# A 90-degree rotation of 96 images: slabs 1 and 2 loaded in 8 KB lines and stored in 16 KB lines

## The chip, the cores and the metric

The kernel runs on one core of a Trainium2 chip. The metric is the device time of one execution in microseconds (us). Before the change the median of three runs is 123.79 us (123.77 to 124.07).

## What is computed

```python
x: float32 [32, 3, 256, 256]
np.rot90(x, k=-1, axes=(-2, -1)).astype(np.float32)
```

Each of the 96 images of 256 x 256 is turned clockwise by 90 degrees: row r of the output is column r of the input, read from the last row up. There is no arithmetic. 25.17 MB are read from HBM and 25.17 MB are written.

## The kernel before

The 96 images make 24576 rows of 1 KB. They are cut into twelve slabs of 2 MB (8 images, 2048 rows); a slab has two halves of 1 MB, `i` = 0 and 1. A slab is loaded into a tile of 128 partitions x 16 KB, turned by VectorE with its transpose of 32 x 32 blocks, and stored from the tile where the turned slab lies, its `home`.

There are two ways to lay a half of a slab on the partitions. In the *short* one each of the 128 partitions has 8 consecutive rows, one line of 8 KB of HBM. In the *long* one each of 64 partitions (every second one, `i::I`) has 16 consecutive rows, one line of 16 KB. The turn takes the one to the other, or, over two slabs at once, long to long:

- Slab 0 (`long_st`) is loaded short (L92, one DMA of 1 MB for each half) and stored long (L130, again one DMA for each half). Its turn (L103 to L106) writes into PSUM; at the very end ScalarE copies it to SBUF (L146) and it is stored last.
- Slabs 1 to 7 are loaded long (L96, one DMA of 1 MB for each half) and stored short (L132, one DMA of 2 MB for both halves). Their turn is at L114 to L116.
- Slabs 8 to 11 are turned in pairs, 8 with 9 and 10 with 11. They are loaded long and stored long: one DMA of 2 MB for the first of a pair (L124) and two of 1 MB for the second (L127).

Slab n is turned into the tile of slab n-1 (`home`, L100), which the turn before has emptied. A slab's turn is two transposes of 128 x 2048 elements, a pair's four (L118).

All DMAs are issued by SP, in program order, into one queue: first every load, in the order 0, 1, 2, 3, 7, 4, 5, 6, 8 to 11, then the stores in the order 4, 3, 5, 6, 7, 1, 2, 8 to 11, 0. Eight completion semaphores are used in turn, so SP waits before the ninth DMA until the first has landed, and so on. The first half of slab 11 is loaded as 14 rows and then 2 rows for each partition; the first store (slab 4's) waits until the 14 rows have landed. Stores otherwise wait for the turn that fills their home. VectorE turns the slabs in the order 0 to 7, then the pair 8 and 9, then the pair 10 and 11.

Of the kernel before, what the change touches and what calls it, by code (L numbers as in the profile page):

```python
# [1 line left out]

# [4 lines left out]

@with_exitstack
def kernel(
    ctx: ExitStack,
    tc: tile.TileContext,
    x: bass.AP,
    out: bass.AP,
):

    nc = tc.nc
    fp32 = mybir.dt.float32

    B, C, H, W = x.shape
    P = nc.NUM_PARTITIONS
    RL, RS = 16, 8  # L50
    I = 2
    Q = P * RS // H
    n_slabs = B * C // (Q * I)
    last = n_slabs - 1
    F = RS * W
    long_st = (0,)
    both = (8, 10)
    paired = [n + a for n in both for a in range(2)]

    rows_in = x.rearrange("b c h w -> (b c h) w")  # L60
    rows_out = out.rearrange("b c h w -> (b c h) w")

    def short(rows):
        return rows.rearrange("(n i p r) w -> n p i (r w)", i=I, p=P, r=RS)

    def long(rows):
        return rows.rearrange("(n i m r) w -> n i m (r w)", i=I, m=P // I, r=RL)

    ld_short, ld_long, st_short, st_long = short(rows_in), long(rows_in), short(rows_out), long(rows_out)

    units = [None] * n_slabs
    adjacent = [(3, 7), (8, 9), (10, 11)]
    pairs = []
    for us in adjacent + [(u,) for u in range(n_slabs) if all(u not in us for us in adjacent)]:
        pool = ctx.enter_context(tc.tile_pool(name=f"unit{us[0]}", bufs=1))
        held = pool.tile([P, len(us), I * F], fp32, name=f"u{us[0]}")
        for j, u in enumerate(us):
            units[u] = held[:, j]
        pairs.append(held)
    psum = ctx.enter_context(tc.tile_pool(name="psum", bufs=1, space=bass.MemoryType.PSUM))  # L80
    turned0 = psum.tile([P, I * F], fp32, name="turned0")

    def fours(t):
        return t.rearrange("p (i f) -> p i f", i=I)

    for n in (0, 1, 2, 3, 7, 4, 5, 6, *range(8, n_slabs)):
        if n in ():
            nc.sync.dma_start(out=fours(units[n]), in_=ld_short[n])
            continue
        for i in range(I):  # L90
            if n in long_st:
                ld = nc.sync.dma_start(out=fours(units[n])[:, i], in_=ld_short[n][:, i])  # L92
            else:
                cuts = (0, 14 * W, RL * W) if (n, i) == (last, 0) else (0, RL * W)
                for f0, f1 in zip(cuts, cuts[1:]):
                    ld = nc.sync.dma_start(out=units[n][i::I, f0:f1], in_=ld_long[n, i][:, f0:f1])  # L96
                    if f1 == 14 * W:
                        mark = ld

    home = [turned0] + units[:last]  # L100

    def turn(n):
        if n in long_st:  # L103
            src = fours(units[n]).rearrange("p i (r g c) -> p c r g i", r=RS, c=RL)
            dst = home[n].rearrange("p (c k r) -> p c r k", c=RL, r=RS)[:, :, ::-1, ::-1]
            parts, step = 2, RL // 2  # L106
        elif n in paired:
            if n not in both:
                return
            src = pairs[both.index(n) + 1].rearrange("p a (r g c) -> p c r g a", r=RL, c=RL)  # L110
            dst = pairs[both.index(n)].rearrange("p i (c k r) -> p c r k i", c=RL, r=RL)[:, :, ::-1, ::-1, :]
            parts, step = 4, RL // 4
        else:
            src = units[n].rearrange("p (r g c) -> p c r g", r=RL, c=RS)  # L114
            dst = fours(home[n]).rearrange("p i (c k r) -> p c r k i", c=RS, r=RL)[:, :, ::-1, ::-1, :]
            parts, step = 2, RS // 2  # L116
        for h in range(parts):
            nc.vector.transpose(out=dst[:, h * step : (h + 1) * step], in_=src[:, h * step : (h + 1) * step])  # L118

    def store(n):  # L120
        if n in paired:
            first = n if n in both else n - 1
            if n == first:
                nc.sync.dma_start(out=st_long[n].transpose([1, 0, 2]), in_=pairs[both.index(n)][::I])  # L124
                return
            for i in range(I):
                nc.sync.dma_start(out=st_long[n, i], in_=pairs[both.index(first)][n - first :: I, i])  # L127
        elif n in long_st:
            for i in range(I):
                nc.sync.dma_start(out=st_long[n, i], in_=home[n][i::I])  # L130
        else:
            return nc.sync.dma_start(out=st_short[n], in_=fours(home[n]))  # L132

    for n in range(both[0]):
        turn(n)
    for n in (4, 3, 5, 6, 7, 1, 2):
        st = store(n)
        if n == 4:
            tc.add_manual_dep(st.ins, mark.ins.name, mybir.DependencyInfo(
                mybir.DependencyClass.Sync, mybir.DependencyReason.SCHED_ONLY), reason="stores after loads")  # L140
    for n in range(both[0], n_slabs):
        turn(n)
        store(n)

    for i in range(I):
        nc.scalar.copy(out=fours(units[last])[:, i], in_=fours(turned0)[:, i])  # L146
    home[0] = units[last]
    store(0)


# [1 line left out]
_INS = ['x']  # L152
_OUTS = [((32, 3, 256, 256), 'float32')]


# [23 lines left out]
```

## Time and profile before

| | |
|---|---|
| median of three runs | 123.79 us (123.77 to 124.07) |
| profiled execution | 123.77 us, its span 122.0 us |
| DMA | 50.33 MB, 97.6% of the span of 16 engines |
| VectorE | 90.5 us busy, 24 transposes |
| ScalarE | 4.9 us busy, two copies of 1.87 us and a table load |
| loads (L92, L96) | 25 DMAs: 23 of 1 MB, one of 896 KB, one of 128 KB |
| stores | 9 DMAs of 2 MB, 6 of 1 MB |
| last store issued, last packet ends | 103.9 us, 120.8 us |

The page divides the span into 40 slices and shows for each engine the busy share in tenths. The DMA row is the mean over the core's sixteen DMA engines; since neighbouring packets overlap by a few ns, a share can come out a little over 100%. A DMA is cut into packets, here one for each line of 8 or 16 KB, and one of 4 bytes for each DMA and engine that reports the completion. A window of the queue gives the packets, the bytes and the share of that stretch. The timeline shows when SP issues a DMA, not when its bytes move.

### The profile page before, as it was taken

The page shows a single profiled execution, that of the slowest core. Times are in us where ns is not written, and L with a number is a line of the kernel's source. Part 1 is how long each engine was busy: PE and PEld are TensorE (multiplying, and loading weights), DVE is VectorE, ACT ScalarE, POOL GpSimd, SP SyncE. Part 2 cuts the span into 40 slices and gives each one's busy share as a digit, 9 for nine tenths or more (in the row PEclk, how much of TensorE's full clock was granted, in tenths as well). Part 3 has the DMA queues.
Part 4 walks back from the last instruction along what each step waited for, and adds up shares of the span by engine and source line. Part 5 has one row for each costly group of instructions (what it writes and reads, how often), then busy time and mean ns, then how long its engine had stood idle before and what let it go on. Part 6 is the DMA issues. An engine that isn't in the chain of part 4 may idle for free.

```text
span 122.0 us, 134 instructions
## 1 busy us (share of the span) xinstructions
DVE 90.5 (74%) x24; ACT 4.9 (4%) x3; POOL 0.2 (0%) x4
## 2 busy tenths in 40 slices
DVE  0039999999999999999999999999999940000000
ACT  0000000000000000000040000000000056000000
POOL 0000000000000000000000000000000000000000
DMA  3999999999999999999999999999999999999993
GB/s 89 427 435 430 430 430 430 430 430 430 430 430 430 430 430 430 430 424 430 429 406 427 430 419 424 430 430 430 416 427 424 451 430 424 424 430 419 419 430 161
DMA packets 4800, 50.33 MB, mean 413 GB/s; under 512 B 640, under 2 KB 640, under 8 KB 704
## 3 DMA queue, kind: packets, MB, share of 16 engines
q1 hardware_dynamic: 4800, 50.33, 97.6%
HBM read 25.17 MB, written 25.17 MB: 413 GB/s over the span
## 4 chain that ended last, share of the span: by engine, by line
DMA 51%; DVE 20%; issue 3%; DVEq 3%; SPq 3%; ACT 2%; ACTq 1%
DMA u<-in_x_dram 45%; DVE u L118 20%; DMA out_dram<-u 6%; DVEq L174 3%; SPq L96 2%; ACT u L146 2%; ACTq L174 1%; SPq L92 1%; DVEq L118 0%; SPq L132 0%
## 5 line engine op out<-in xcount | busy, mean ns | idle before, releaser
L118 DVE STREAM_TRANSPOSE u<-u 128x2048 f32<-128x2048 f32 x22 | 83.4, 3850 | 0.3
L118 DVE STREAM_TRANSPOSE turned<-u 128x2048 f32<-128x2048 f32 x2 | 7.1, 3584 | 8.1 <-DMA u<-in_x_dram 8.1
L146 ACT COPY u<-turned 128x2048 f32<-128x2048 f32 x2 | 3.6, 1868 | 35.7 <-DVE u L118 35.7
L146 ACT ACT_TABLE_LOAD x1 | 1.3, 1283 | 62.0 <-DMA u<-in_x_dram 62.0
L163 POOL MEMSET const-bfloat16-1.0<- 128x1 bf16 x1 | 0.1, 102 | 0.0
L163 POOL MEMSET const-uint8-127<- 128x1 uint8 x1 | 0.1, 101 | 0.0
L163 POOL MEMSET const-float32-0.0<- 128x1 f32 x1 | 0.1, 99 | 0.2 <-issue 0.2
L163 POOL MEMSET const-float32-1.0<- 128x1 f32 x1 | 0.1, 98 | 0.0
## 6 DMA issues: line engine op xcount, KB each, us to landing
u<-in_x_dram SPq DMA_DIRECT2D x23, 1024.0 KB, 19.6
out_dram<-u SPq DMA_DIRECT2D x9, 2048.0 KB, 16.6
out_dram<-u SPq DMA_DIRECT2D x6, 1024.0 KB, 16.7
u<-in_x_dram SPq DMA_DIRECT2D x1, 896.0 KB, 19.3
u<-in_x_dram SPq DMA_DIRECT2D x1, 128.0 KB, 17.1
```

The costliest lines, as they stand in the source:

```text
L92: ld = nc.sync.dma_start(out=fours(units[n])[:, i], in_=ld_short[n][:, i])
L96: ld = nc.sync.dma_start(out=units[n][i::I, f0:f1], in_=ld_long[n, i][:, f0:f1])
L118: nc.vector.transpose(out=dst[:, h * step : (h + 1) * step], in_=src[:, h * step : (h + 1) * step])
L146: nc.scalar.copy(out=fours(units[last])[:, i], in_=fours(turned0)[:, i])
L163: nc = _bacc.Bacc("TRN2", target_bir_lowering=False, num_devices=1)
L174: with _tile.TileContext(nc) as tc:
```

## The change

Slabs 1 and 2 join slab 0 in `long_st`, so that they are loaded short and stored long. Each of their loads is one DMA of 2 MB in 8 KB lines (L88), in place of two of 1 MB in 16 KB lines (L96). Each of their stores is two DMAs of 1 MB in 16 KB lines (L130), in place of one of 2 MB in 8 KB lines (L132). Their turn takes slab 0's form (L103 to L106), into SBUF. Order of slabs, homes, waits and everything else are as before.

```diff
-    long_st = (0,)
+    long_st = (0, 1, 2)
...
     for n in (0, 1, 2, 3, 7, 4, 5, 6, *range(8, n_slabs)):
-        if n in ():
+        if n in (1, 2):
             nc.sync.dma_start(out=fours(units[n]), in_=ld_short[n])
             continue
```

## The prediction

> **What bounds the kernel now.** I read the page first, then windows of the DMA queue, then VectorE's and SP's timelines. The first question was who is busy to the end.
>
> ```profile
> span 122.0 us, 134 instructions
> DVE 90.5 (74%) x24; ACT 4.9 (4%) x3; POOL 0.2 (0%) x4
> DVE  0039999999999999999999999999999940000000
> DMA  3999999999999999999999999999999999999993
> DMA packets 4800, 50.33 MB, mean 413 GB/s; under 512 B 640, under 2 KB 640, under 8 KB 704
> q1 hardware_dynamic: 4800, 50.33, 97.6%
> ```
>
> The sixteen DMA engines are busy in every slice but the first and the last. VectorE stops at about slice 32. The chain of waits names VectorE and ScalarE near the end, but it follows issues: the last store is issued at 103.9 us and its last packet ends at 120.8, because everything before it still stands in the queue. So the end is set by the sum of the packets. The span is then a ramp of 1.8 us before the first packet, 119.1 us of packets, and 1.2 us of closing. A change of line size acts here only through what a packet costs, or by letting the queue run dry.
>
> The second view is the queue in five windows, each pure in one kind of packet: 8 KB loads (slab 0), 16 KB loads early (most of slabs 1, 2 and 3), 16 KB loads late, 8 KB stores (slabs 6, 7, 1 and most of 2), and the final 16 KB stores.
>
> ```profile
> DMA packets 103, 0.84 MB, mean 422 GB/s; under 512 B 0, under 2 KB 0, under 8 KB 0
> q1 hardware_dynamic: 103, 0.84, 99.5%
> ...
> DMA packets 526, 7.05 MB, mean 440 GB/s; under 512 B 96, under 2 KB 96, under 8 KB 96
> q1 hardware_dynamic: 526, 7.05, 103.0%
> ...
> q1 hardware_dynamic: 1041, 13.65, 100.2%
> ...
> q1 hardware_dynamic: 994, 7.66, 101.3%
> ...
> q1 hardware_dynamic: 685, 9.39, 100.5%
> ```
>
> The windows are 5.2 to 7.2, 8 to 24, 24 to 56, 76 to 94 and 97 to 119 us. Share times window times 16, divided by the packets, gives a packet's mean; the 4-byte packets (those under 512 B, 9 ns each) are taken off. An 8 KB load packet is 309 ns, a 16 KB one 611 (early) and 614 (late); an 8 KB store packet 312, a 16 KB one 615 to 616. Neighbours on one engine overlap by some ns, so I also sorted the packet records into the sixteen engines and took the time from one DMA's last packet to the next one's. Per MB: 8 KB loads 2.453 us, early 16 KB loads 2.434, later ones 2.447, 16 KB stores 2.434 at best and 2.456 usually. A 2 MB store in 8 KB packets takes 4.900 us at best. The stores of slabs 1 and 2 took 4.976 and 4.981 at the last engine: they ran when the engines had fallen out of step (the completions of one DMA spread over 0.34 us at 66 us and over 0.73 us or more from 86 us on).
>
> The third view is what could starve the queue.
>
> ```profile
> 8.11 7.08 DVE L118 STREAM_TRANSPOSE turned<-u 128x2048 f32<-128x2048 f32 x2 [8.11 <-DMA u<-in_x_dram]
> 15.22 7.80 DVE L118 STREAM_TRANSPOSE u<-u 128x2048 f32<-128x2048 f32 x2
> 70.06 3.07 SPq L132 DMA_DIRECT2D out_dram<-u  x3
> 84.50 0.70 SPq L124 DMA_DIRECT2D out_dram<-u  x1
> 98.91 0.63 SPq L124 DMA_DIRECT2D out_dram<-u  x1
> 102.57 2.67 SPq L130 DMA_DIRECT2D out_dram<-u  x2
> ```
>
> Each of these store issues waits for VectorE or ScalarE. The queue still holds work then: at 70.06 to 81.3 us, at 84.50 to 96.3 (the last 8 KB packet's end), at 98.91 to 106.1, at 102.57 to 115.9. The smallest cover is 7.2 us, or 6.1 after the 1.06 us that the first load took from issue to first packet.
>
> **The change, part by part.** Durations are those of the profiled execution, 123.77 us beside a span of 122.0. The median of the three runs, 123.79, is 0.02 above it, which I add at the end.
>
> Removed: four 1 MB loads in 16 KB packets (slabs 1 and 2). Added: two 2 MB loads in 8 KB packets. Per engine that is 32 packets of 8 KB for 16 of 16 KB. By the times per MB: 4 x (2.453 - 2.434) = +0.076 us. By packet means: 16 x (2 x 309 - 611) = +0.112. I take 0.08, since the time from DMA to DMA counts the overlap. No row shows a load that takes two 8 KB pieces a partition from places 1 MB apart, as these do; the stores of L132 have that order, and their ends are my bounds: 4.900 us at best, 5.085 at the last engine for the worst one (slab 5's), so from +0.06 to +0.43 for the two. Nearest is slab 0's own 8 KB load, which reads the same kind of line.
>
> Removed: two 2 MB stores in 8 KB packets (slabs 1 and 2). Added: four 1 MB stores in 16 KB packets. At the place in question: 4.976 + 4.981 = 9.957 us goes, and 4 x 2.456 = 9.824 comes, so -0.13. At best paces of both, 2 x 4.900 against 4 x 2.434, it is -0.06; at a 2.475 that one 16 KB store took, -0.06 too. I take -0.13, the rows nearest in time.
>
> Completion packets: two DMAs fewer in loading, two more in storing, 9 ns each per engine: 0.
>
> SP's issues: four loads at 0.57 to 0.62 us become two, and nothing waits for them, since the queue had work from 1.8 us on. Later, two store issues that took 1.27 and 1.32 us become four of the L130 kind (1.24 and 1.38). SP, at 70.5 us, is busy until about 75.8 in place of 73.1; behind them on SP stands only the store of slab 8, which VectorE releases at 84.50. Cost 0, cover 8.7 us. The eight completion lanes, which SP waits on before reusing one, shift by two in the loads and back in the stores; each lane reused after 70 us then belongs to a DMA landed by about 96 us at the latest, none later than before. Cost 0.
>
> VectorE: four transposes change from the 16-row form (3.91 to 3.98 us for these slabs) to slab 0's form, which took 3.61 and 3.56 into PSUM. Into SBUF with that step no row shows it; 3.56 and 3.98, the ends of all transposes here, bound it, so VectorE's end moves by -1.5 to +0.2 us. I take -1.4, and it is worth 0: VectorE is ahead of the queue by 7 us or more at every store. If it were slow instead, the cover of 6.1 us would be spent at 1.5 us more per transpose. Slab 1 must be there when VectorE comes at 15.2 us; its load ends at about 12.6 as before.
>
> Sum: 123.77 + 0.08 - 0.13 + 0.02 = 123.74 us.
>
> One rule speaks against half of this. The Trainium skill, page "DMA: Bandwidth & Descriptors", section "Rules for kernel authors", says that two transfers to disjoint partition halves aren't worth it, since both spread over the same 16 engines, and to use one 128-partition transfer; its section on the anatomy of a DMA puts a fixed 2.0 us on each. If those 2.0 us stood in line here, two more stores would cost an estimated 4.0 us. In this trace back-to-back half-partition stores follow each other at 2.46 us per MB, no slower than the 128-partition ones, so by the row the sum keeps 0.
>
> **The rivals.**
> *A, slower: the new loads put the engines out of step from the start.* The 2 MB stores did this between 66 and 91 us. For it: they have the order that the new loads have. Against it: the first of them (slabs 4 and 3) ran at 4.90 to 4.98 on all engines, and loads so far stay in step. Price in the mild case: two loads at 4.98 in place of 4 x 2.434, +0.22, and the 18 MB of loads behind them at 2.456, two of these 0.022 more than now and the rest 0.010, +0.20; with the stores' -0.13 the net is +0.29 and the time 124.08. With loads at 5.085 it is 124.29. It decides from +0.37 net, so from 5.02 us a load.
> *B, faster: the engines stay in step longer.* If the disorder is bred by 8 KB stores, five in place of seven breed less, and the 16 KB stores run at 2.434. The ten MB of 16 KB stores from 96.27 to 120.83 us, 24.56 us, become 24.34, and the replaced pair's 9.957 become 9.736: -0.44, with the loads' +0.08 -0.36, so 123.43. Against it: the disorder was there at 86 us, before the replaced stores.
> *C, the queue runs dry.* VectorE late by more than 6.1 us: each us beyond costs one. No transpose in the trace is near 1.5 us over another.
> *D, the halves cost.* A visible fixed cost per added store, bounded by the slowest 16 KB MB: 2 x 0.02 = 0.04 us. Below notice.
>
> **How the numbers follow.** About 0.3% (0.37 us) is what a measurement of this kernel tells from no change. The forecast has 0.72, A 0.14, B 0.09, C 0.01, and 0.04 is for what none of these names. Slower by over 0.3% is half of A, C and three quarters of the rest, 0.11; faster is most of B and the last quarter of the rest, 0.08; "same" is left with 0.81. The forecast's own range is 123.55 (stores at their best and no loss on loads) to 123.95 (loads at twice the cost and no gain on stores). For 8 in 10 it reaches into both A and B: 123.4 to 124.2.
>
> **What the changed profile would show.** Right: the queue again busy in every slice; an 8 KB load packet of 309 to 311 ns between 7 and 17 us; last load packet about 0.08 us later than 58.95; 8 KB packets gone after 86 us, 16 KB ones at 615 in their place; four transposes near 3.6 us; SP's four issues over by 76 us. Wrong: 8 KB loads at 315 ns or more, or 16 KB loads above 616 (A); a DMA slice under 9 in the store half (C); the final 16 KB stores at 611 (B).

## The result

| | before | after |
|---|---|---|
| median (6 runs each, side by side) | 123.81 us (123.53 to 124.07) | 123.21 us (123.14 to 123.44) |
| ratio after to before, 95% interval | | 0.9953 [0.9938, 0.9968] |
| profiled execution, its span | 123.77, 122.0 us | 123.21, 121.4 us |

The change makes the kernel faster by 0.47%. The forecast was 123.74 us and no change that can be told (123.4 to 124.2). A later set of runs on another occasion (the kernel after again, below) gave less: 123.22 against 123.59 us, 0.9977 [0.9963, 0.9990].

### The profile page after: what moved, and what is told of

The parts are those of the page before. It is cut to its first block, busy times and chain, and to the rows that moved or that the text cites. A ratio compares the mean times of both kernels' runs of the same rounds, so it can differ in the third digit from the quotient of the medians.

```text
span 121.4 us, 134 instructions
## 1 busy us (share of the span) xinstructions
DVE 90.5 (75%) x24; ACT 4.9 (4%) x3; POOL 0.2 (0%) x4
## 4 chain that ended last, share of the span: by engine, by line
DVE 55%; issue 17%; DMA 6%; DVEq 3%; ACT 2%; ACTq 1%; SPq 0%
DVE u L118 50%; DVE turned L118 6%; DMA u<-in_x_dram 6%; DVEq L174 3%; ACT u L146 2%; ACTq L174 1%; SPq L92 0%; DVEq L118 0%
```

## The profile after

The page of the kernel after, its parts 1 to 3:

```profile
span 121.4 us, 134 instructions
DVE 90.5 (75%) x24; ACT 4.9 (4%) x3; POOL 0.2 (0%) x4
DVE  0029999999999999999999999999999960000000
DMA  3999999999999999999999999999999999999994
DMA packets 4800, 50.33 MB, mean 414 GB/s; under 512 B 640, under 2 KB 640, under 8 KB 704
q1 hardware_dynamic: 4800, 50.33, 98.0%
```

The same number of packets, the same bytes, and again no slice of the DMA row below 9 but the first and the last. So the queue never ran dry in either kernel, and what the change saved is time per packet. VectorE and SP in the kernel after, from its timeline (start, duration, what):

```profile
15.36 15.68 DVE L118 STREAM_TRANSPOSE u<-u 128x2048 f32<-128x2048 f32 x4
59.46 11.13 SPq L132 DMA_DIRECT2D out_dram<-u  x5
70.64 5.49 SPq L130 DMA_DIRECT2D out_dram<-u  x4
84.66 0.65 SPq L124 DMA_DIRECT2D out_dram<-u  x1
102.76 2.67 SPq L130 DMA_DIRECT2D out_dram<-u  x2
```

SP's four new store issues end at 76.1 us and the next one starts at 84.66, when VectorE releases it: nothing waits there, as forecast. The queue itself, in windows of 8 to 17 us (8 KB loads of slabs 1 and 2), 18 to 56 (16 KB loads), 64 to 84 (8 KB stores that the change doesn't touch) and 97 to 119 (16 KB stores that it doesn't touch):

```profile
DMA packets 482, 3.82 MB, mean 424 GB/s; under 512 B 16, under 2 KB 16, under 8 KB 16
q1 hardware_dynamic: 482, 3.82, 100.2%
...
q1 hardware_dynamic: 1238, 16.35, 101.1%
...
DMA packets 1108, 8.55 MB, mean 428 GB/s; under 512 B 64, under 2 KB 64, under 8 KB 64
q1 hardware_dynamic: 1108, 8.55, 101.0%
...
DMA packets 690, 9.47 MB, mean 430 GB/s; under 512 B 112, under 2 KB 112, under 8 KB 112
q1 hardware_dynamic: 690, 9.47, 100.6%
```

Before, two of these windows, 64 to 84 and 97 to 119 us:

```profile
q1 hardware_dynamic: 1106, 8.54, 101.2%
...
DMA packets 685, 9.39 MB, mean 427 GB/s; under 512 B 112, under 2 KB 112, under 8 KB 112
```

Share times window times 16, less 9 ns for each 4-byte packet, over the packets that are left: the unchanged 8 KB stores went from 310.2 to 309.0 ns a packet, the unchanged 16 KB ones from 615.6 to 610.9. The packet records say it more sharply: in the kernel after every 8 KB store packet between 64 and 86 us takes exactly 309 ns, and all but 11 of its 896 16 KB store packets take 611. Stores at these two prices, 309 and 611 ns, are called clean below; stores whose packets take longer are said to collide, a name for what is seen, since the profile doesn't show what makes a packet longer. Sorted into the sixteen engines, the completions of one DMA are spread over 0.448 us at 66.6 us and over the same 0.448 still at 115.4: the engines go on in a fixed relation to one another, and none falls behind. In the kernel before, the spread grows from 0.34 to 0.75 us over the same time.

The ledger, from the packet records (a stretch ends with the last engine's completion; us):

| stretch | before | after | difference |
|---|---|---|---|
| slab 0 loaded, at | 7.64 | 7.83 | +0.19 |
| loads of slabs 1 and 2 | 9.78 | 9.80 | +0.02 |
| the other 18 MB of loads | 44.00 | 44.07 | +0.08 |
| stores of slabs 4, 3, 5, 6, 7 (unchanged) | 24.90 | 24.50 | -0.40 |
| stores of slabs 1 and 2 | 9.96 | 9.74 | -0.22 |
| the last 10 MB of stores (unchanged) | 24.56 | 24.33 | -0.23 |
| last completion, at | 120.83 | 120.27 | -0.56 |

The sum is the whole difference between the two profiled executions, 123.77 - 123.21 = 0.56 us. Three quarters of the gain in the stores (0.63 of 0.85 us) lie in stores that the change leaves alone.

## The experiments

Three theories were put up. L: the loads of slabs 1 and 2 leave the sixteen engines in another relation to one another, and in it the stores don't collide. S: the stores of slabs 1 and 2 in 8 KB packets breed the collisions (the forecast's rival B). C: each execution draws its pace by chance.

**The kernel before once more.** No edit.

> The kernel before, unchanged, for a second profile. What is asked: is the slow pace of its stores (up to 4.98 us for 2 MB in 8 KB packets, 2.456 us a MB in 16 KB packets) a property of the kernel or of one execution? Theory L (the loads of slabs 1 and 2 leave the engines in a relation to one another in which the stores collide) and theory S (the stores of slabs 1 and 2 in 8 KB packets bring the collisions) both expect it again: final 16 KB stores at 615 ns a packet, 123.8 us. Theory C (a new draw in each execution) expects another pattern, anywhere from 611 to 616 ns, and a time between 123.2 and 124.1.

Measured: 123.70 us, 1.0003 [0.9990, 1.0017] of before. The window of 97 to 119 us of this second profile:

```profile
DMA packets 682, 9.34 MB, mean 425 GB/s; under 512 B 112, under 2 KB 112, under 8 KB 112
q1 hardware_dynamic: 682, 9.34, 100.0%
```

That is 615.8 ns a packet, and the stretches of the ledger's stores are 24.90, 9.98 and 24.55 us, nearly those of the first profile. The slow pace belongs to the kernel in both executions that were profiled. It may not be fixed, though: the 90 runs of before beside the experiments lie between 123.00 and 124.00 us, and only profiled executions show their pace, so that some of these may have run clean. An estimate from the ledger: a kernel with before's loads and wholly clean stores would take 123.77 - 0.40 - 0.16 - 0.23 = 122.98 us (0.16: two stores at 4.90 for 9.96).

**The new loads alone.**

```diff
-        if n in ():
+        if n in (1, 2):
```

> The new loads of slabs 1 and 2 alone (two of 2 MB in 8 KB lines); turns and stores as before. The rows of these two slabs so come out in another order than the reference's. Theory L: the stores run clean, 8 KB packets at 309 ns and 16 KB ones at 611, the stores of slabs 1 and 2 at 4.90 us each; loads end 0.3 us later than before, stores take 0.8 us less; 123.3 us. Theory S: stores collide as before and the loads cost 0.1 to 0.3 us; 123.9 to 124.1 us. Theory C: no pattern.

Measured: 123.48 us, 0.9981 [0.9970, 0.9993]. The window of 97 to 119 us:

```profile
DMA packets 693, 9.52 MB, mean 433 GB/s; under 512 B 112, under 2 KB 112, under 8 KB 112
q1 hardware_dynamic: 693, 9.52, 101.3%
```

It moves 9.52 MB where before moves 9.39, at 612.0 ns a packet. The store stretches (the ledger's three rows on stores) are 24.52, 9.80 and 24.33 us, with the 8 KB stores of slabs 1 and 2 still in place. The loads end at 61.64 us against 61.41. So the loads alone bring the clean stores, as theory L has it, and S falls as the main cause.

The last packet ends at 120.30 us, only 0.02 after that of the kernel after, but the span is 121.7 against 121.4. With two DMAs fewer the last store's semaphore comes earlier in the order in which SP waits for the eight at the close, and two waits follow it, 0.06 us each. The last store also reported 0.09 us later after its packet than in the kernel after.

**The new loads alone, in as many DMAs as before.**

```diff
-            if n in long_st:
+            if n in (0, 1, 2):
                 ld = nc.sync.dma_start(out=fours(units[n])[:, i], in_=ld_short[n][:, i])
```

> The new line size of the loads alone, in as many DMAs as before (40, four loads of 1 MB in 8 KB lines), turns and stores as before; the rows of slabs 1 and 2 come out in another order than the reference's. With 38 or 42 DMAs the last store's semaphore was followed by two more waits of SP at the close, about 0.06 us each in the profile; with 40 it comes last, as in the kernels before and after. If that is the difference, this run is 0.12 us under the run with the new loads alone: 123.36 us, stores clean (309 ns) as there. If the time stays at 123.48, the closing waits don't matter.

Measured: 123.28 us (123.25 to 123.42) beside 123.59, 0.9981 [0.9972, 0.9991]. The window of 97 to 119 us:

```profile
DMA packets 692, 9.50 MB, mean 432 GB/s; under 512 B 112, under 2 KB 112, under 8 KB 112
q1 hardware_dynamic: 692, 9.50, 101.1%
```

Store stretches 24.53, 9.80 and 24.33 us, and a span of 121.5. The median is 0.31 us below before's, that of the 38-DMA form was 0.17 below; the two ratios are the same, so the close's part is seen in the profile and not settled by the runs.

**The new turn and stores alone.**

```diff
-    long_st = (0,)
+    long_st = (0, 1, 2)
...
-            if n in long_st:
+            if n == 0:
                 ld = nc.sync.dma_start(out=fours(units[n])[:, i], in_=ld_short[n][:, i])
```

> The new turn and stores of slabs 1 and 2 alone (four of 1 MB in 16 KB lines); loads as before. The rows of these two slabs so come out in another order than the reference's. Theory L: the five 8 KB stores ahead collide as before, 16 KB packets at 615 ns; 123.7 us. Theory S: 16 KB packets at 611 ns from 86 us on and no load cost; 122.9 to 123.2 us. Theory C: no pattern.

Measured: 123.59 us (123.16 to 123.75), 0.9989 [0.9975, 1.0003]: no difference that the interval tells. The window of 97 to 119 us:

```profile
DMA packets 687, 9.42 MB, mean 428 GB/s; under 512 B 112, under 2 KB 112, under 8 KB 112
q1 hardware_dynamic: 687, 9.42, 100.6%
```

614.1 ns a packet; store stretches 24.78, 9.84 and 24.55 us. The collisions remain, also in the last 10 MB, after five 8 KB stores in place of seven. The replaced pair itself gains 0.12 us, what the forecast's term said (-0.13). Of its two closing waits (42 DMAs) the same holds as above.

**Two loads of 1 MB a slab, in the kernel after.**

```diff
-        if n in (1, 2):
+        if n in ():
```

> The kernel after with the 8 KB loads of slabs 1 and 2 issued as two DMAs of 1 MB each, as slab 0's are; turns and stores as after. It tells the line size of these loads from the 2 MB form. If the 8 KB lines set the engines' relation to one another, the stores run clean again (16 KB packets at 611 ns in the end, 123.2 us). If it is the 2 MB form with its two places a partition, or SP's shifted lanes, the stores collide as before (615 ns, 123.6 to 123.8 us).

Measured: 123.42 us, 0.9982 [0.9964, 1.0000]. Store stretches 24.51, 9.74 and 24.34 us: clean. So the 8 KB lines do it without the 2 MB form. Its last packet ends at 120.30 us, like that of the kernel after, and its span is again 121.7: 42 DMAs.

**Slab 0 in one load, all else as before.**

```diff
-        if n in ():
+        if n in (0,):
```

> The kernel before with slab 0's load as one DMA of 2 MB in the same 8 KB lines; all else is unchanged, so no packet's size changes and only the order of slab 0's packets at the very start does. Theory L in a narrow form (it takes the 8 KB lines of slabs 1 and 2): 123.8 us, stores colliding as before. Theory S: 123.8 us. Theory C, or a form of L in which any other start gives another relation of the engines: the stores' pace changes with it, to anywhere between 123.2 and 124.1 us.

Measured: 123.70 us, 1.0000 [0.9989, 1.0011]. The time is before's, and the window of 97 to 119 us shows collisions, 614.2 ns a packet:

```profile
DMA packets 688, 9.44 MB, mean 429 GB/s; under 512 B 112, under 2 KB 112, under 8 KB 112
q1 hardware_dynamic: 688, 9.44, 100.8%
```

But the ledger has changed. The loads end at 61.86 us, 0.45 later than before's, and 0.39 of it stand at slab 0. Then the five unchanged 8 KB stores take 24.50 us at the last engine in place of 24.90, and slab 1's takes 4.90; only from slab 2's on (4.96 us) is the slow pace back, with 24.57 us for the last 10 MB. So another start alone does change the stores, as the wide form of theory L has it; what it brings is lost in the loads, and it doesn't last. The six stores aren't clean either: 8 to 12% of their packets take longer than 309 ns, but the engine that ends last isn't held up. A collision costs time only where it hits that engine.

**Slabs 5 and 6 in place of 1 and 2.**

```diff
-    long_st = (0,)
+    long_st = (0, 5, 6)
...
-        if n in ():
+        if n in (5, 6):
```

> The kernel before with slabs 5 and 6 in the new form in place of 1 and 2: their 8 KB loads come at 31 to 41 us, their 16 KB stores at 71 to 81 us. The same packets in all, at another place. If 8 KB loads anywhere ahead of the stores give the good relation: stores clean, 123.2 us. If only the early place does it: stores collide, 123.6 to 123.8 us.

Measured: 123.59 us (123.33 to 123.86), 0.9991 [0.9980, 1.0003]. The window of 97 to 119 us, 615.8 ns a packet:

```profile
DMA packets 686, 9.40 MB, mean 427 GB/s; under 512 B 112, under 2 KB 112, under 8 KB 112
q1 hardware_dynamic: 686, 9.40, 100.7%
```

8 KB stores take 311.5 ns a packet from 80 to 90 us and 312.8 after that. At the last engine, though, the stores of slabs 4, 3, 5, 6 and 7 take 24.44 us, which is 3 x 4.90 and 4 x 2.434, and slab 1's 4.90; slab 2's takes 4.97, the last 10 MB 24.55. The loads end at 61.77 us, 0.36 later than before's. So the same packets at a later place free the first stores too, pay for it in the loads, and the collisions are back before the end.

**Slab 1 alone.**

```diff
-    long_st = (0,)
+    long_st = (0, 1)
...
-        if n in ():
+        if n in (1,):
```

> The change for slab 1 alone (8 KB load, 16 KB stores); slab 2 as before. If the good relation comes with any early 8 KB load: stores at 309 and 611 ns, 123.3 us. If it takes both: stores collide, 123.55 to 123.7 us. Halfway in time with a pace between would mean that it is a matter of chance in each execution.

Measured: 123.29 us (123.10 to 123.68) beside 123.59, 0.9984 [0.9972, 0.9997]. Store stretches in the profile: 24.50, 9.77 and 24.49 us, at the last engine clean at first and slow again in the last 10 MB. One early 8 KB load does most of it in this profile. The ten runs reach from the clean kernels' times to before's, so that the chance of an execution (theory C) may have a part in it; one profile doesn't tell.

**The first stores held back (three kernels).** The aim was to let the queue run empty once between loads and stores, in the kernels before and after:

```diff
-                    if f1 == 14 * W:
+                    if f1 > 14 * W:
                         mark = ld
```

> The kernel before, but the first store waits for the whole of slab 11's load, not for 14 of 16 rows of its first half, so the queue runs empty once between loads and stores. The theory that the stores' pace is carried over from the loads by the engines' relation to one another: the sixteen engines restart, the history is erased, and this kernel's store pace equals that of the next run's, whichever it is. The gap costs 2 to 3 us: 125.5 to 126.7 us. If the pace belongs to something else that the loads leave behind, this kernel has 615 ns in its final 16 KB stores and the next one 611.

> The kernel after with the same drain between loads and stores. Relation carried by the engines: the same store pace as in the run just before, within 1 ns a packet while the same packets run (the five 8 KB stores). Other carrier: 309 ns here and over 310 there. Time 125.2 to 126.5 us.

and, since a store had moved ahead, with a second store held:

```diff
-        if n == 4:
+        if n in (4, 3):
```

> The kernel before with both of the first two stores waiting for the whole of slab 11's first half, last of the loads but one, so that no store is issued earlier than before. (In the runs meant to drain the queue, the store of slab 3 had moved ahead of the waiting one.) The engines are not restarted here: the wait is 0.3 us longer than before, less than what is queued. If the stores' pace is carried over by the engines, it collides as before: 615 ns, 123.6 to 123.9 us. If the mere later issue makes it clean, 611 ns and 123.1.

None of them did what it was meant to. The held stores wait for the very last load (the third expectation was wrong on that too), and in each kernel another store moved ahead of them: slab 3's in the first two, slab 5's in the third. SP's timeline of the third and its queue from 58.8 to 61.8 us, when the last MB is loaded:

```profile
54.41 18.50 SPq L132 DMA_DIRECT2D out_dram<-u  x7
...
DMA packets 98, 1.07 MB, mean 357 GB/s; under 512 B 20, under 2 KB 20, under 8 KB 23
q1 hardware_dynamic: 98, 1.07, 95.3%
```

The queue holds one store from 54.41 us on and never empties, but it moves 357 GB/s while the last MB of loads is under way (411 before), and the engines take 2.45 to 3.19 us for it, where all took 2.46 before. So the engines entered the stores in another relation, spread over 0.59 us in place of 0.36. The same in the first two (0.77 and 0.91 us). Then this, from 97 to 119 us of the third:

```profile
DMA packets 688, 9.44 MB, mean 429 GB/s; under 512 B 112, under 2 KB 112, under 8 KB 112
q1 hardware_dynamic: 688, 9.44, 100.3%
```

611.2 ns a packet. The store stretches:

| kernel | five stores | slabs 1 and 2 | last 10 MB | time, us | ratio |
|---|---|---|---|---|---|
| before, slab 3's store ahead | 24.51 | 9.80 | 24.33 | 123.54 | 0.9997 [0.9980, 1.0014] |
| after, slab 3's store ahead | 24.50 | 9.74 | 24.33 | 123.52 | 0.9991 [0.9976, 1.0006] |
| before, slab 5's store ahead | 24.50 | 9.80 | 24.33 | 123.61 | 1.0003 [0.9991, 1.0016] |

With before's loads, and with all seven 8 KB stores, every packet from the second store on takes 309 or 611 ns, once the engines have been shaken at the end of the loads. Time is not gained, since the slow last MB costs 0.5 to 0.8 us, most or all of what clean stores give before. But it shows that the loads of slabs 1 and 2 aren't needed for a clean pace, and that 8 KB stores don't breed collisions by themselves. All these runs fit one reading: how the engines stand to one another when the stores begin decides. It isn't shown apart from the rest, since in these three kernels one store also runs ahead of its place.

**The kernel after once more.** No edit.

> The kernel after, unchanged, beside these runs on one chip and for a second profile. Stores clean again at 309 and 611 ns, loads ending 0.3 us later than before's, 123.2 us, 0.9965 of before.

Measured: 123.22 us (123.10 to 123.57) beside 123.59, 0.9977 [0.9963, 0.9990]. Store stretches 24.50, 9.74 and 24.37 us; the loads end 0.18 us later than in the second profile of before, 0.05 of it at slab 0, 0.09 at slabs 1 and 2, 0.04 behind them.

Put together, by the last set, with one before (123.59): the new loads 123.28, the whole change 123.22 us. The loads give 0.31 us net of the 0.37. The last 0.06 is less than the runs can tell (the two intervals overlap); it is what, by the profiles, four 16 KB stores of 1 MB at 2.434 us save on two 8 KB stores at 4.90 when both run clean (9.80 - 9.74).

Over all profiles: in the three with before's loads and no store held (before twice, the new stores alone) the stores of slabs 4, 3, 5, 6 and 7 take 24.78 to 24.90 us; in all eleven others 24.50 to 24.53 (24.44 with slabs 5 and 6 in the new form). That leaves little room for theory C in these first stores. What lies ahead of the stores sets their first pace; whether that pace lasts to the end differs.

## Why the prediction was wrong

- **The bound** was read rightly: the queue is full from end to end, and the 0.56 us between the profiles are time of packets. (The forecast's lower end, 123.55, leaves out the 0.02 us that its sum adds: 123.57.)
- **The loads' term**, +0.08 us, was about right at the two loads themselves: +0.02 in the ledger, +0.09 between the two second profiles. The 8 KB loads of slab 1 run at 4.90 us for 2 MB, the price that the forecast took from slab 0; in slab 2's 16% of the packets already collide, without holding up the last engine (4.90). All the loads together end 0.29 and 0.18 us later. 0.08 and 0.04 of it come behind slabs 1 and 2, which the sum put at nothing; 0.19 and 0.05 stand at slab 0, whose packets the change doesn't touch, and that is chance as far as the record shows: the same load ended at 7.61 to 7.79 us in the other profiles.
- **The stores' term** is the step that failed: "4.976 + 4.981 = 9.957 us goes, and 4 x 2.456 = 9.824 comes, so -0.13". It took the collisions in the rows before as given, priced only the replaced stores, and put every store that isn't in the diff at nothing. The stores gained 0.85 us: 0.22 in the replaced pair, 0.63 in the others. What brought it, by the runs, is the new loads ahead of them: alone they make the same stores clean, and the new stores alone gain 0.12 in the pair.
- **Rival B** named the state that came true (16 KB stores at 2.434 us, the replaced pair at 9.736) and was given 0.09. It came true by luck: its reason, fewer 8 KB stores, was wrong, since with only the stores changed the collisions stay, and with only the loads changed they go. The argument held against it, "the disorder was there at 86 us, before the replaced stores", is true and proved nothing, because the change also acts earlier, through the loads. For the same reason its price stopped at 123.43 us: it left out the 0.40 us of the five first stores.
- **Rival A** looked at the right place, the new loads as what sets the engines' relation, and took the opposite sign for granted. The loads behind slabs 1 and 2 did get slower as it said, but by 0.08 us, not 0.20.
- **VectorE**: the four transposes were taken at 3.6 us, by slab 0's rows into PSUM. Into SBUF the same form took 4.01 and 3.97 us; the four take 15.68 us as against 15.66. It cost nothing, as argued; the price was off by 1.4 us.
- **SP's issues, completion packets, rivals C and D**: as forecast, 0.
- **The Trainium skill's rule** on partition halves ("DMA: Bandwidth & Descriptors", "Rules for kernel authors"): set aside on the row, rightly. The four half-partition stores of slabs 1 and 2 take 2.434 us a MB here, 9.74 in all, less than two 128-partition ones at 4.90, whose lines are half as long. The fixed 2.0 us that the prediction sets beside it stand in that page's section on DMAs issued by GpSimd, while SP issues these; no such cost shows in this queue.

What stays open: which property of the sixteen engines' relation makes the stores collide or not, and why 8 KB lines in the loads of slabs 1 and 2 give a pace that lasts (or nearly, in the second profile of the kernel after), while those of slabs 5 and 6, of slab 1 alone, or slab 0 in one load, give one that is lost before the end. The spread of the engines doesn't tell: stores that stayed clean began with spreads from 0.22 to 0.91 us, those that collided at once with 0.33 to 0.36, those that lost their pace later with 0.67 to 0.89. The profile has no engine number on its packets, so that it isn't known which engines hinder which. No kernel was tried that sets the relation at no cost; by the estimate above, clean stores behind before's own loads would be worth 122.98 us.

## What to carry to other kernels

Where one queue is full all the time, a packet's price isn't a constant of its size: compare its mean with the smallest one in the trace, and take the difference, over all packets of the stage, as what any change of the traffic ahead may give or take. Here that was 0.8 us, six times the term that was argued over. A range should reach to that floor, and a chance should not be talked away from it by an order of events in the one kernel that has been profiled. Compare whole stretches from the first packet to the last: a run whose time doesn't move can hide a gain in one stage that another has eaten, as slab 0's one load does.

## What was not expected of the hardware

- Sixteen DMA engines ran all their stores, some 59 us, with 8 KB packets at 309 ns and nearly every 16 KB packet at 611, or, in the same stores behind other loads, with means of up to 313 and 618 ns a store. Which of the two it was at the start went with what lay ahead of the first store; in three profiles the pace was lost later.
- Packets that took longer on engines with slack cost nothing: six 8 KB stores in a row took 4.90 us each while 8 to 12% of their packets were over 309 ns (slab 0 in one load).
- A single store queued early behind the loads, with the next ones held, slowed the last MB of loads from 2.46 us to as much as 3.25 on some engines. Why was not tried.
- A 128x2048 transpose of the same form took 3.56 to 3.61 us into PSUM and 3.97 to 4.01 us into SBUF.
- Which of SP's eight semaphores the last DMA uses shows at the close: with two waits still behind it, the span ended 1.37 and 1.39 us after the last packet, in place of 1.16 in the kernel after; of that 0.06 us for each wait, the rest in the later report of the last store. The report alone varies as much: 1.24 us in the run with the new loads in 40 DMAs, where no wait follows.
